# Reordering the attention work inside a fused decoder layer: scores, casts, row copies and meta rows at other steps

## The chip, the cores and the metric

The kernel runs on one core of a Trainium2 chip. The metric is the device time of one execution in microseconds (us). A core has a matmul engine (TensorE, PE in the profile; its weight loads are listed apart as PEld), a vector engine (DVE), a scalar engine (ACT), a general engine (POOL) and a queue for transfers (SP). Each of them works through its own list of instructions in order, and waits at an instruction until what it needs is there. SBUF is the working memory (rooms and raw, hi and lo buffers in the profile's names); PSUM holds the results of matmuls, and its eight banks are used here as four for sums that build up over many matmuls ("acc") and four for everything short ("ps").

## The reference

One step of one layer of a decoder, in float32, for a prompt of 512 tokens behind 16 meta tokens and for 8 running sequences of 4 new tokens each, which have 256 tokens in a paged cache:

```
h = x + 0.5 * rms_norm(swiglu(rms_norm(x), ffn1))
u = rms_norm(h);  proj = u @ w_in            # q,k,v,r and gates of both branches
o_a = gla(q_a, k_a, v_a, g)                  # gated linear attention, in chunks of 64
o_b = sb_attend(q_b, k_b, v_b, bias)         # stick-breaking attention, 16 heads of 64
m = sigmoid(gate_a) * (o_a @ w_o_gla) + sigmoid(gate_b) * (o_b @ w_o_sb)
h = h + rms_norm(m @ w_out)
y = h + 0.5 * rms_norm(swiglu(rms_norm(h), ffn2))

# sb_attend: z = q.k / 8 + bias, keys strictly before the query
# A[t,s] = sigmoid(z_ts) * prod over s<j<t of (1 - sigmoid(z_tj)),  out = A @ v
```

D_MODEL is 1024. Results are y for prompt and samples, the new rows of k and v, and the state of the linear attention.

## The kernel before, in words

**Products.** Every float32 operand of a large product is split into a high part (a cast, on ACT) and a low part (what is left, a subtraction on DVE, line 172). A product is then three matmuls: hi by hi, hi by lo, lo by hi. The wide projections are done with seven block products instead of eight (`seven_steps`, L1049 to L1084): the four accumulators a, d, b and c get sums of several products each, and two of them start from a copy of another: b from a, and c from b. These two copies (L1069, ACT) are called **seeds** here. Copies L1059 take intermediate values out of accumulators. The seven products come in the order a, d, b, d, c, a, c; their weights are four sets of blocks, named b1, t, b2 and t4, each with a cast (L1006 for hi) and a subtraction (lo) at dates that `weights_at` (L1041) hands out.

**Order.** PE, DVE, ACT and POOL run in an order that is written by hand; only SP's transfers are placed by the framework. The clock of that order is `step()` (L745), called once every six matmuls of a projection; `later(n, f)` does f n steps on. The attention has eight pairs of heads. Projections of pair p+1 take 22 steps: eight for the queries (L728 to L731), fourteen for keys and values (`seven_steps`, lines L1079 to L1081). The attention proper of pair p is laid between them, at step numbers that a table gives:

- `scores(n)` for three tiles of queries: six matmuls (L1997) into two PSUM banks, one for each head; a little later two sigmoids for each head out of the bank (L2004, L2005, ACT); POOL sets a few columns to zero.
- `scan` (L2021, DVE), the running product, and `weigh` (L172 and L2031, DVE), the weights, for two parts of the row and both heads: 815 columns for tiles 0 and 1, 528 for tile 2.
- `rows_k` and `rows_v`: k and v of the pair are turned (four transposes each, L2039 and L2054), copied out of PSUM (L2043 and L2058, both ACT) and sent out.
- `tails` (L2067 and on) and `turned` (L2096, copies L2099): the weights are transposed; `summed` (L2112) multiplies them with v; `meta_turned` (L2122, a cast L2123 on ACT and a subtraction on DVE) and `meta_summed` (L2127) add what the meta tokens give.
- In pairs 4 to 7 `sample_keys` (L2199, copies L2201) turns cached keys of the running sequences in four groups of four transposes, a PSUM bank each, and `sample_products` (L2213) multiplies with them. `sample_rows_out` (L2178) is done once.

The casts and subtractions of the next pair's queries (L1928 and on) are laid there too. After the pairs comes the mixer, whose value r is done by `seven_steps` again; `by_t` and `by_sg` work on its output (L2410), and `split` (L2352) casts it to hi.

**Rooms.** Most SBUF buffers come from one arena; where each `take` is put, a table of bytes says (PLACES, L53), one byte for each take in the order of the program. A room is taken anew as soon as `give` returned it, and the next writer waits for the last reader.

## Time and profile before

| | us |
|---|---|
| time, three runs | 1498.48, 1499.78, 1499.94 |
| median | 1499.78 |
| the profiled execution | 1498.65 |
| its span, first to last instruction | 1496.9 |
| PE busy in the span | 1477.6 |
| DVE, ACT, POOL busy | 1081.4, 804.8, 59.0 |

The attention pairs lie between about 587 and 825 us of the span; a plain pair's 22 steps take about 27.6 us, a pair with sample keys 32.1. In the profile a row of the timeline gives start, duration, engine, line, operation, output and input, the number of like instructions in a row, and in brackets the idle time of the engine just before it with what ended it. "PE ps L2199 <- ACT room L2043" in the list of waits is PE's line 2199, waiting for ACT's line 2043. Matmuls of 280 columns follow each other every 0.13 us, though each has a row of 0.29: their rows overlap.

### The profile page before, as it was taken

How to read it: one execution, taken by the hardware profiler on the slowest of the kernel's cores; microseconds unless marked ns; L12 is line 12 of the kernel's file. 1: busy time of each engine (PE TensorE's matmuls, PEld its weight loads, DVE VectorE, ACT ScalarE, POOL GpSimd, SP SyncE). 2: the span in 40 equal slices, each digit the busy share in tenths (PEclk: the TensorE clock that was granted, in tenths of full speed). 3: DMA queues.
4: the chain of work that ended last, by engine and by line, in shares of the span. 5: the costliest groups of instructions: out<-in, count | busy, mean ns of one | idle time of the engine just before them, and what ended most of it. 6: DMA issues, size and time to landing. Idle time of an engine off the chain costs nothing.

```text
span 1496.9 us, 29837 instructions
## 1 busy us (share of the span) xinstructions
PE 1477.6 (99%) x11905; PEld 1423.7 (95%) x11905; DVE 1081.4 (72%) x1820; ACT 804.8 (54%) x1513; POOL 59.0 (4%) x175
## 2 busy tenths in 40 slices
PE   9999999999999999999899999999999999999998
PEld 8999999999999889888789899999999999999998
DVE  5888888855676866877766844766567898888544
ACT  6455444533655656766766543644565555455333
POOL 2000000000000011200100000000000000000000
PEclk9999999999999999999999999999999999999999
DMA  8133333224655586556566857344531333333252
GB/s 252 51 91 100 99 96 102 86 79 139 164 138 142 158 157 163 118 125 131 129 126 169 245 139 212 90 103 129 171 103 66 99 100 99 99 101 94 82 174 93
DMA packets 288542, 187.61 MB, mean 125 GB/s; under 512 B 10989, under 2 KB 266675, under 8 KB 288403
## 3 DMA queue, kind: packets, MB, share of 16 engines
q1 hardware_dynamic: 280706, 181.97, 44.2%
q0 software_dynamic: 7680, 3.74, 2.4%
q8 instruction: 93, 1.52, 0.4%
q14 instruction: 47, 0.38, 0.1%
q10 hardware_dynamic: 16, 0.00, 0.0%
HBM read 160.63 MB, written 25.03 MB: 124 GB/s over the span
## 4 chain that ended last, share of the span: by engine, by line
PE 90%; DVE 3%; ACT 2%; DMA 2%; issue 1%; SPq 1%; DVEq 0%; ACTq 0%
PE acc L1300 8%; PE acc L1302 8%; PE acc L1301 8%; PE acc L741 6%; PE acc L742 6%; PE acc L744 6%; PE acc L728 5%; PE acc L729 4%; PE acc L731 4%; PE acc L1079 4%; PE acc L1081 3%; PE acc L1080 3%; DVE room L172 1%; PE acc L1242 1%; PE acc L1239 1%; PE acc L1240 1%
## 5 line engine op out<-in xcount | busy, mean ns | idle before, releaser
L172 DVE TENSOR_TENSOR room<-room,room 128x280 f32<-128x280 f32 (+13 forms) x462 | 288.2, 643 | 84.0 <-ACT room L808 18.3
L172 DVE TENSOR_TENSOR lo<-raw,hi 128x1024 fp32r<-128x1024 f32 (+1 forms) x207 | 248.1, 1199 | 98.0 <-ACT hi L1006 60.3
L1300 PE MATMUL acc<-room,hi 128*128 128x280 f32 (+1 forms) x896 | 260.0, 290 | 0.0
L1302 PE MATMUL acc<-room,lo 128*128 128x280 f32 (+1 forms) x896 | 259.7, 290 | 0.0
L1301 PE MATMUL acc<-room,hi 128*128 128x280 f32 (+1 forms) x896 | 259.5, 290 | 0.0
L1006 ACT CAST hi<-raw 128x1024 fp32r<-128x1024 f32 x114 | 119.6, 1053 | 141.5 <-PE acc L1301 49.5
L728 PE MATMUL acc<-room,hi 128*128 128x280 f32 x608 | 172.9, 301 | 0.3 <-DVE room L175 0.3
L1300 PEld LDWEIGHTS acc<-room,hi 128*128 128x128 f32 x896 | 168.7, 188 | 0.0
L1302 PEld LDWEIGHTS acc<-room,lo 128*128 128x128 f32 x896 | 168.6, 188 | 0.0
L1301 PEld LDWEIGHTS acc<-room,hi 128*128 128x128 f32 x896 | 168.6, 188 | 0.0
L729 PE MATMUL acc<-room,hi 128*128 128x280 f32 x608 | 163.6, 288 | 0.0
L1079 PE MATMUL acc<-room,hi 128*128 128x280 f32 x476 | 142.8, 300 | 3.2 <-ACT acc L1069 3.0
L172 DVE TENSOR_TENSOR lo<-room,hi 128x1024 fp32r<-128x1024 f32 x106 | 101.3, 955 | 56.5 <-ACT hi L1006 56.3
L1081 PE MATMUL acc<-room,lo 128*128 128x280 f32 (+1 forms) x476 | 138.6, 291 | 0.8 <-DVE lo L172 0.8
L1080 PE MATMUL acc<-room,hi 128*128 128x280 f32 (+1 forms) x476 | 138.4, 291 | 0.0
L706 ACT CAST hi<-raw 128x1024 fp32r<-128x1024 f32 (+1 forms) x93 | 93.6, 1007 | 74.4 <-issue 21.4
L1006 ACT CAST hi<-room 128x1024 fp32r<-128x1024 f32 x106 | 88.9, 839 | 82.3 <-PE acc L1301 60.1
L731 PE MATMUL acc<-room,lo 128*128 128x280 f32 x608 | 125.9, 288 | 0.0
L728 PEld LDWEIGHTS acc<-room,hi 128*128 128x128 f32 x608 | 114.4, 188 | 5.4 <-issue 3.8
L729 PEld LDWEIGHTS acc<-room,hi 128*128 128x128 f32 x608 | 114.6, 188 | 0.6
L741 PE MATMUL acc<-room,hi 128*128 128x280 f32 (+2 forms) x388 | 110.7, 295 | 0.0
L742 PE MATMUL acc<-room,hi 128*128 128x280 f32 (+2 forms) x388 | 108.8, 290 | 0.0
(404 smaller groups left out, 3515.8 us busy)
## 6 DMA issues: line engine op xcount, KB each, us to landing
raw<-in_w_in_dram SPq DMA_DIRECT2D x68, 256.0 KB, 5.2
raw<-in_ffn_w_gate_dram SPq DMA_DIRECT2D x64, 256.0 KB, 3.1
raw<-in_ffn_w_up_dram SPq DMA_DIRECT2D x64, 256.0 KB, 3.4
raw<-in_ffn_w_down_dram SPq DMA_DIRECT2D x36, 448.0 KB, 4.0
raw<-in_w_in_dram SPq DMA_DIRECT2D x29, 512.0 KB, 7.0
out_dram<-room SPq DMA_DIRECT2D x36, 256.0 KB, 6.2
room<-in_cache_k_dram SPq DMA_DIRECT2D x32, 256.0 KB, 6.7
room<-in_cache_v_dram SPq DMA_DIRECT2D x32, 256.0 KB, 5.2
```

Of the source, the lines that this page charges most:

```text
L172: (eng or V).tensor_tensor(out=out, in0=a, in1=b, op=op)
L728: T.matmul(acc[h][:, :w], hi[k], act.get(k, h, w)[0], start=(k == order[0]), stop=False, skip_group_check=True)
L729: T.matmul(acc[h][:, : wid[h]], hi[k], a[h][1], start=False, stop=False, skip_group_check=True)
L731: T.matmul(acc[h][:, : wid[h]], lo[k], a[h][0], start=False, stop=(k == order[-1]), skip_group_check=True)
L741: T.matmul(acc[h][:nw, : wid[h]], wh, a[h][0], start=(k == 0), stop=False)
L742: T.matmul(acc[h][:nw, : wid[h]], wh, a[h][1], start=False, stop=False)
L1006: S.copy(hi[:, :kt], src)
L1079: T.matmul(x[:, :n], hi, act_[k][0][:, :n], start=(first and k == 0), stop=False, skip_group_check=True)
L1081: T.matmul(x[:, :w], lo, act_[k][0][:, :w], start=False, stop=(k == 3), skip_group_check=True)
L1300: T.matmul(x[:, :QW], hi, act[k][0], start=(first and k == 0), stop=False, skip_group_check=True)
L1301: T.matmul(x[:, :QW], hi, act[k][1], start=False, stop=False, skip_group_check=True)
L1302: T.matmul(x[:, :QW], lo, act[k][0], start=False, stop=(k == 3), skip_group_check=True)
```

## The change

No instruction is added or taken away. The table of steps and a few dates change, the copy of the k rows goes from ACT to DVE, and the table of places is replaced as a whole.

```diff
-            for n, f in ((3, samples), (6, hi), (9, lo)):
+            for n, f in ((3, samples), (8, hi), (10, lo)):
...
         def rows_k(self):
...
                 kt = take(512)
-                S.copy(kt, p)
+                V.tensor_copy(kt, p)
...
-                later(4, lambda: give(kt))
-            later(3, out)
+                later(10, lambda: give(kt))
+            later(2, out)
...
         def rows_v(self):
...
-            later(4, out)
+            later(3, out)
...
         def meta_summed(self):
             T.matmul(self.op, once["vm"][:NR], once["az"][:NR], start=False, stop=True)
             o, pr = take(NP), self.pr
-            S.copy(o, self.op)
-            later(3, lambda: nc.sync.dma_start(ob_dram[pr], o))
-            later(7, lambda: give(o))
+            def out():
+                S.copy(o, self.op)
+                later(2, lambda: nc.sync.dma_start(ob_dram[pr], o))
+                later(6, lambda: give(o))
+            later(1, out)
...
         def by_sg(i):
             tt(o[i], o[i], sg[i], ALU.mult)
             give(t[i], sg[i])
-            split(oas, n + i, o[i], oap)
+            later(2, lambda: split(oas, n + i, o[i], oap))
...
-    SK, SP, TURN = (14, 14, 14, 14), (16, 16), (17, 17, 17, 20, 20, 20)
+    SK, SP, TURN = (14, 14, 14, 14), (19, 19), (16, 16, 16, 19, 19, 19)
...
-            now, n, after = Pair(pr), BEGIN[pr + 1], BEGIN[pr + 2] if pr < 7 else BEGIN[8] + 22
+            now, n, after = Pair(pr), BEGIN[pr + 1], BEGIN[pr + 2] if pr < 7 else BEGIN[8] + 21
             if pr >= PLAIN:
-                weights_at(then, BEGIN[pr] + TILE, ("kv", pr), (-6, -6, -5, -4), t=(-3, -2), b2=(2, 3), t4=(5, 7))
+                weights_at(then, BEGIN[pr] + TILE, ("kv", pr), (-6, -6, -5, -4), t=(-3, -1), b2=(0, 3), t4=(7, 9))
...
-            pieces = [(3, now.scores, 0), (3, now.scores, 1), (4, now.meta), (6, now.scan, 0, 0), (7, now.scan, 1, 0),
-                      (8, now.scan, 0, 1), (9, now.weigh, 0, 0), (10, now.scan, 1, 1), (12, now.weigh, 1, 0),
-                      (11, now.scores, 2), (11, now.rows_v), (11, now.rows_k),
-                      (14, now.scan, 0, 2), (15, now.weigh, 0, 1), (16, now.scan, 1, 2), (17, now.weigh, 1, 1), (17, now.tails)]
-            pieces += [(TURN[i], now.turned, i // 3, i % 3) for i in range(6)] + [(TURN[5], now.meta_turned)]
+            pieces = [(3, now.scores, 0), (3, now.scores, 1), (4, now.meta), (5, now.scan, 0, 0), (6, now.scan, 1, 0),
+                      (7, now.scan, 0, 1), (8, now.weigh, 0, 0), (9, now.scan, 1, 1), (11, now.weigh, 1, 0),
+                      (10, now.scores, 2), (10, now.rows_v), (10, now.rows_k),
+                      (12, now.scan, 0, 2), (13, now.weigh, 0, 1), (14, now.scan, 1, 2), (15, now.weigh, 1, 1), (16, now.tails)]
+            pieces += [(TURN[i], now.turned, i // 3, i % 3) for i in range(6)]
...
+            then(after + 1, now.meta_turned)
             then(after + 1, now.summed)
             then(after + 1, now.meta_summed)
...
-        then(BEGIN[2] + 14, sample_rows_out)
+        then(BEGIN[2] + 21, sample_rows_out)
```

Two places show what this makes of the engines' lists. The first is ACT in the pair at 699 to 731 us, the first one with sample keys, from the first seed (L1069) to the second. L2004 and L2005 are the sigmoids of the last tile, a couple for each head; L1059 copies the value e5; "ps" with a number is a PSUM bank. Before:

```order
L1069 COPY acc_8195<-acc_8193 128x280
L1006 CAST hi_8225<-raw_7900 128x1024
L1059 COPY room_76_4272<-acc_8194 128x280
L2004 ACTIVATE room_7_75<-ps_8238,sbb 128x512
L2005 ACTIVATE room_76_4272<-ps_8238,sbb 128x512
L2004 ACTIVATE room_79_4590<-ps_8239,sbb 128x512
L2005 ACTIVATE room_103_5552<-ps_8239,sbb 128x512
L1006 CAST hi_8282<-room_98_5485 128x512
L1928 CAST room_44_452<-room_60_3148 128x512
L1069 COPY acc_8196<-acc_8195 128x280
L1059 COPY room_75_4271<-acc_8195 128x280
L2043 COPY room_60_3148<-ps_8251 128x512
```

And now (L2205 is the line of the sample keys' copies, which was L2201):

```order
L1069 COPY acc_8202<-acc_8200 128x280
L2004 ACTIVATE room_91_5265<-ps_8230,sbb 128x512
L2005 ACTIVATE room_5_73<-ps_8230,sbb 128x512
L1059 COPY room_71_4267<-acc_8201 128x280
L2004 ACTIVATE room_71_4267<-ps_8231,sbb 128x512
L2005 ACTIVATE room_124_7976<-ps_8231,sbb 128x512
L2058 COPY room_9_112<-ps_8238 128x512
L1069 COPY acc_8203<-acc_8202 128x280
L1059 COPY room_124_7976<-acc_8202 128x280
L2205 COPY room_91_5265<-ps_8301 128x512
L2205 COPY room_99_5529<-ps_8307 128x512
L2205 COPY room_9_112<-ps_8313 128x512
```

The first head's sigmoids now stand ahead of L1059, the b2 cast (L1006, 128x1024) ahead of the first seed, and the casts L1006 (128x512, the t4 blocks) and L1928 behind the sample keys; L2058 stands where L2043 did not, ahead of the second seed, and L2043 has left this list.

The second place is DVE in the first pair, from the subtraction for the t blocks (lo, first row) to the scan of the last tile (128x528). Before:

```order
L172 TENSOR_TENSOR lo_6773<-room_86_4753,hi_6772 128x1024
L2021 SCALAR_TENSOR_TENSOR room_60_3148<-room_60_3148,room_74_4270 128x416
L2021 SCALAR_TENSOR_TENSOR room_104_5553<-room_104_5553,room_74_4270 128x400
L172 TENSOR_TENSOR room_103_5552<-room_103_5552,room_104_5553 128x815
L2031 COPY room_95_5301<-room_103_5552 128x6x16
L2021 SCALAR_TENSOR_TENSOR room_60_3148<-room_60_3148,room_74_4270 128x400
L1924 COPY room_94_5276<-room_98_5485 64x4x4 x4
L172 TENSOR_TENSOR lo_6824<-raw_6375,hi_6823 128x1024
L172 TENSOR_TENSOR room_79_4590<-room_79_4590,room_60_3148 128x815
L2031 COPY room_95_5301<-room_79_4590 128x6x16
L2021 SCALAR_TENSOR_TENSOR room_104_5553<-room_104_5553,room_74_4270 128x528
```

And now:

```order
L172 TENSOR_TENSOR lo_6774<-room_5_73,hi_6773 128x1024
L172 TENSOR_TENSOR room_9_112<-room_9_112,room_100_5549 128x815
L2031 COPY room_98_5501<-room_9_112 128x6x16
L2021 SCALAR_TENSOR_TENSOR room_71_4267<-room_71_4267,room_79_4672 128x400
L1924 COPY room_98_5501<-room_5_73 64x4x4 x4
L172 TENSOR_TENSOR room_49_871<-room_49_871,room_71_4267 128x815
L2031 COPY room_98_5501<-room_49_871 128x6x16
L172 TENSOR_TENSOR lo_6804<-raw_6375,hi_6803 128x1024
L2043 COPY room_99_5529<-ps_6839 128x512
L2021 SCALAR_TENSOR_TENSOR room_100_5549<-room_100_5549,room_79_4672 128x528
```

Two scans have gone ahead of the first row, the other head's 815-column product ahead of the second subtraction, and the k rows' copy L2043 stands behind that subtraction, ahead of the last tile's scan.

## The prediction

> **What bounds the kernel now.** I read the page's totals first, then PE's waits, then the timeline around each wait, on PE and on the engine that releases it.

> ```profile
> span 1496.9 us, 29837 instructions
> PE 1477.6 (99%) x11905; PEld 1423.7 (95%) x11905; DVE 1081.4 (72%) x1820; ACT 804.8 (54%) x1513; POOL 59.0 (4%) x175
> ```

> PE is busy 99% of the span. The change takes no instruction away from it, so it can give back only part of the 1496.9 − 1477.6 = 19.3 us in which PE stood idle, and what hides behind the busy figure. Which of that idle time belongs to the attention pairs, the list of PE's waits tells (columns: total us, times, longest):

> ```profile
> PE ps L2199 <- ACT room L2043: 4.4, 3, 1.5
> PE acc L1079 <- ACT acc L1069: 3.0, 3, 1.0
> PE ps L2199 <- ACT room L2005: 1.5, 3, 0.5
> PE acc L1081 <- DVE lo L172: 0.8, 1, 0.8
> PE ps L2122 <- DVE room L172: 0.6, 1, 0.6
> PE ps L2178 <- ACT room L2005: 0.2, 1, 0.2
> ```

> These are 10.5 us, and all of them have an instruction that the change moves as releaser. They are shown too small: a matmul's own row is longer than the pitch at which matmuls follow each other. So I measure each stall as distance between neighbours on PE, less what the distance would be undisturbed. First the sample-key transposes (L2199), which pairs 4 to 6 put into PE's stream:

> ```profile
> 711.52 0.29 PE L1081 MATMUL acc<-room,lo 128*128 128x280 f32 x1
> 711.92 0.66 PE L2199 MATMUL ps<-ident,room 128*128 128x128 f32 x4
> 713.07 0.66 PE L2199 MATMUL ps<-ident,room 128*128 128x128 f32 x4 [0.50 <-ACT room L2005]
> 715.19 1.14 PE L2199 MATMUL ps<-ident,room 128*128 128x128 f32 x8 [1.47 <-ACT room L2043]
> 716.09 0.37 PE L1079 MATMUL acc<-room,hi 128*128 128x280 f32 x1
> 716.31 0.29 PE L1080 MATMUL acc<-room,hi 128*128 128x280 f32 x1
> 716.44 0.29 PE L1081 MATMUL acc<-room,lo 128*128 128x280 f32 x1
> ```

> From the last projection matmul to the next are 716.09 − 711.52 = 4.57 us. Four transposes more make a group 1.14 − 0.66 = 0.48 longer, so sixteen need 1.92; with the pitch of 0.13 (716.44 − 716.31) and some 0.1 to enter the block that is 2.15. Lost: 2.4 us, three times. What holds them is ACT's queue:

> ```profile
> 710.30 0.39 ACT L1059 COPY room<-acc 128x280 f32<-128x280 f32 x1 [2.07 <-PE acc L1081]
> 710.59 0.69 ACT L2004 ACTIVATE room<-ps,sbb 128x512 f32<-128x512 f32 x1
> ...
> 712.31 0.71 ACT L2005 ACTIVATE room<-ps,sbb 128x512 f32<-128x512 f32 x1
> 712.88 0.65 ACT L1006 CAST hi<-room 128x512 fp32r<-128x512 f32 x1
> 713.39 0.66 ACT L1928 CAST room<-room 128x512 fp32r<-128x512 f32 x1
> 713.91 0.43 ACT L1069 COPY acc<-acc 128x280 f32<-128x280 f32 x1
> ...
> 714.51 0.63 ACT L2043 COPY room<-ps 128x512 f32<-128x512 f32 x1
> ```

> The reader should see the bracket in the first row: ACT stands 2.07 us idle in front of L1059, which needs a product that PE has not finished, with four sigmoids, two casts, the second seed (L1069) and the copy out of PSUM (L2043) lined up behind it. PE then waits for the end of that line, because the four PSUM banks of the scores and rows come free only there. Pairs 2 and 3 have no sample keys; there the same line ends in the seed, and PE waits for that:

> ```profile
> 657.75 0.29 PE L1081 MATMUL acc<-room,lo 128*128 128x280 f32 x1
> 659.08 0.40 PE L1079 MATMUL acc<-room,hi 128*128 128x280 f32 x1 [1.04 <-ACT acc L1069]
> ```

> 1.33 apart instead of 0.13: 1.20 lost, twice.

> **The change, part by part.** *Pairs 4 to 6.* The scores come one step of six matmuls earlier (0.78), and the first head's two sigmoids stand ahead of L1059, in the 2.07 idle us, which hold two at a pitch of 0.57. Behind L1059 remain two sigmoids, from 710.59 to about 711.8 with the second one's tail, then L2058 (the other rows copy) until about 712.4, then the seed. L2043 is no longer in this queue; DVE does it, at about 711. PE wants the four banks at 711.8, 712.2, 712.7 and 713.1 (0.48 a group). The tightest has some 0.3 us left. The casts L1006 and L1928 (0.5 each by their pitch) stand behind the seed, and their readers come four to five steps later. Term: 3 × −2.4 = **−7.2**, bounds −7.5 and, if one bank stays 0.5 late, −5.7.

> *Pairs 2 and 3.* Of what stood between L1059 and the seed, two sigmoids and two casts go (2.2 us) and one copy (0.5) comes: the seed starts near 657.0, ends near 657.4. It is also needed later, since tails and turned rows (L2067, L2096), once behind step 17, now precede its first matmul by well over 1 us. Term: 2 × −1.2 = **−2.4**, with 2 us in hand.

> *The first pair.* Its lost time hangs on DVE:

> ```profile
> 593.79 1.23 DVE L172 TENSOR_TENSOR lo<-room,hi 128x1024 fp32r<-128x1024 f32 x1 [2.24 <-ACT hi L1006]
> 594.94 1.90 DVE L2021 TENSOR_TENSOR_SCAN room<-room,room 128x416 f32<-128x416 f32 x2
> ...
> 599.46 1.22 DVE L172 TENSOR_TENSOR lo<-raw,hi 128x1024 fp32r<-128x1024 f32 x1
> ```

> PE waits 0.8 for the last row's subtraction and 0.6 for the meta rows (L2122); with the 0.16 that a row's length hides (1.20 lost against 1.04 shown, above) these are 0.96 and 0.76. The two scans move ahead of the earlier subtraction, into the 2.24 us that DVE is idle. The weights' product of the other head (1.0) comes ahead of the last subtraction in their place, so this one starts near 598.7 and ends near 599.9, 0.76 sooner: 0.2 remain. L2122 goes into the next pair's sums, where its rows are long finished: its 0.76 go. What is late next: the turned rows' fourth group needs the last tile's weights, and from 599.9 DVE's line of rows copy (0.6), scan (1.25) and product (0.7) ends near 602.45, where PE, by its new order, is ready near 601.95: +0.5. Term: −0.76 − 0.76 + 0.5 = **−1.0**, bounds −1.7 and +0.3.

> *Rows copy on DVE.* The trace has that shape on DVE:

> ```profile
> L2219 DVE COPY room<-ps x2: 666/669/672, 719.5 to 837.7; 128x512 f32<-128x512 f32 x2
> 671.80:699.40 27.60, 26.56 (x216) 24.14 (x214) 21.79 (x39) 19.09 (x38) 3.26 (x10) 1.00 0.82 154
> ```

> 0.67 us against ACT's 0.63. A pair's period (second row: length; PE, PEld, DVE, ACT, POOL busy) has DVE busy 21.79 of 27.60; 22.5 still fits. In pair 2 the line behind it is this, and it has the same durations in the first:

> ```profile
> 657.35 1.25 DVE L2021 TENSOR_TENSOR_SCAN room<-room,room 128x528 f32<-128x528 f32 x1
> 658.70 0.71 DVE L172 TENSOR_TENSOR room<-room,room 128x528 f32<-128x528 f32 x1
> ```

> Going through DVE's new order with these durations, this product ends at about 658.1 instead of 659.4; PE's fourth group wants it at about 658.4. I cost the copy at nothing; PE's early arrival is what could uncover it (rival two). [...]

> *The gate value r.* A seed of the mixer waits behind a cast that waits for DVE:

> ```profile
> 855.29 0.64 ACT L2352 CAST room<-room 128x544 fp32r<-128x544 f32 x1 [1.70 <-DVE room L172]
> 855.84 0.39 ACT L1069 COPY acc<-acc 128x280 f32<-128x280 f32 x1
> 856.28 0.40 PE L1079 MATMUL acc<-room,hi 128*128 128x280 f32 x1 [0.92 <-ACT acc L1069]
> ```

> The cast moves two steps back, behind that seed, which can then start when its source is there. Term: 0.92 and the hidden 0.16, **−1.1**.

> *Smaller ones.* The sample rows (L2178) go seven steps later: **−0.4** (0.2 shown, 0.16 of it hidden as above). The sample products join the second block of turned rows:

> ```profile
> 717.61 0.29 PE L1081 MATMUL acc<-room,lo 128*128 128x280 f32 x1
> 717.83 1.07 PE L2213 MATMUL ps<-room,room 128*32 128x256 f32 x16
> ```

> Entering a block costs 0.22 − 0.13 = 0.09, leaving it the same (716.31 − 716.09 = 0.22). Four blocks less: −0.7 at most, nothing at least; **−0.5**. The meta rows:

> ```profile
> L2123 ACT CAST room<-ps x8: 582/605/607, 609.7 to 821.0; 96x512 fp32r<-96x512 f32 x8
> 611.93 1.94 PE L2112 MATMUL ps<-room,room 128*64 128x512 f32 x10
> ```

> Between their transposes and the matmul that closes the sums PE now has L2112's sixteen, of which ten take 1.94; the cast (0.6) on ACT and a remainder on DVE, as wide as the 0.71 product at most, lie under them: nothing, as long as neither engine is in a longer piece just then. The lo, hi and t4 dates move by one or two steps under three or more of slack: nothing. DMAs: the same ones, earlier by a step; only a kept room (ten steps instead of four) could make a taker wait, and the new table of places goes with it: nothing, with a rival.

> *The clock.* Behind the third stall the windows show this (length; busy and counts of PE, PEld, DVE, ACT, POOL; clock; DMA):

> ```profile
> 775.90:779.30 3.40, 1.39 (x9) 0.84 (x8) 3.23 (x6) 3.40 (x9) 0.20 (x2) 1.00 0.20 42
> 779.30:782.80 3.50, 3.44 (x16) 3.44 (x17) 0.36 (x1) 2.64 (x6) 0.00 (x0) 0.52 0.20 66
> ```

> PE was busy 1.39 of 3.40 us, and in the next 3.5 the granted clock is 0.52: half the work, 1.7 us lost. The first two stalls were as long and had no such stretch. If the idle window goes, I expect the stretch to go with it: **−1.7**, bounds −1.7 and 0. [...]

> Sum: −7.2 − 2.4 − 1.0 − 1.1 − 0.4 − 0.5 − 1.7 = **−14.3 us**. The profiled execution took 1498.65 (span 1496.9 and 1.75 around it), so 1484.35. The median of the three runs is 1499.78, 1.13 higher; I predict against it: **1485.5 us**.

> **Rivals.** *One: the half-clock stretch stays,* or falls in another place. For: the granted clock fell once, and nothing above shows what decides; sixteen transposes in a row remain. Against: no other stretch in the pairs. 1485.5 + 1.7 = 1487.2.

> *Two: DVE's line becomes the releaser.* The waits on ACT go, but PE reaches the turned rows sooner than the last tile's weights, or the end of the sums sooner than the meta rows' remainder. For: 0.3 us in hand in pair 2, DVE 80% busy, one more copy in its line. Against: in pairs 4 to 6 the sample keys give it 2 us more. One lo subtraction of 1.23 in the wrong place, less 0.3 of slack, in seven pairs: 6.5 us back, 1492.

> *Three: part of the bank wait stays.* L2199 then waits for L2058 or the second head's sigmoids: 1.2 in each of three pairs, and the clock's 1.7 stay with it: 1490.8.

> *Four: nothing comes of it.* Rooms of the new table have their last reader later than the old ones, and what came sooner in the order waits for its room. For: the kept room, all places new. Against: every term above was a wait for a bank or for a queue, never for a room. 1499.

> *Five, slower: the rows copy blocks DVE.* It stands ahead of scan and weights and waits itself for PE and for a room that a transfer out reads. If it is held until the b lo and t4 lo subtractions behind it are late at L1081, PE waits in all eight pairs. It decides from about 3 us of delay, what the t4 piece has in hand (four steps of 0.78); for a loss over the 14.3 it must cost 1.8 a pair. At 2.2 a pair: 1485.5 + 17.6 = 1503. Against: its bank's matmuls (L2039) end over 1 us before DVE is there.

> **How the numbers follow.** Forecast 0.60 (its own range 1483 to 1488.5), rival one 0.13, two 0.11, three 0.07, four 0.05, five 0.04. The range must reach rivals one to three: 1482 to 1492; the lower end is the sum with all bounds on the good side (−0.3, −0.7, −0.2), a median no higher than the profiled execution (−1.1), and 1.2 for stalls that I counted too small. A measurement here can tell 0.2%, 3.0 us, from no change. The forecast and rivals one to three are all past that, 0.91, and a sliver of rival four: faster 0.92, same 0.04, slower 0.04.

> **What would show it.** In the changed profile the rows "L2199 <- L2043", "L2199 <- L2005" and "L1079 <- L1069" are missing from PE's waits, and L2199's sixteen stand together in about 2 us; ACT's idle in front of L1059 is under 1 us, with two sigmoids ahead of it; no slice between 700 and 860 us has a clock of 0.5. If PE shows waits of L2096 for DVE in more than the first pair, rival two is right; L2199 with waits of about 1 us, rival three; the same waits as now, four; L1081 waiting for L172 in most pairs, five. I am wrong if PE's idle time falls by under 6 us.

## The result, and the profile after

The changed kernel takes 1483.04 us (median of four runs, 1482.95 to 1483.10); the kernel before, in four runs beside it, 1499.13 (1498.35 to 1499.94). The ratio is 0.9893, with a 95% interval of 0.9875 to 0.9910: 16.1 us faster. The forecast was 1485.5 us, in a range of 1482 to 1492.

The first rows of the changed kernel's page, and from its list of PE's waits the two in the upper rows that are new:

```profile
span 1481.4 us, 29840 instructions
PE 1472.0 (99%) x11905; PEld 1421.1 (96%) x11905; DVE 1086.3 (73%) x1828; ACT 800.6 (54%) x1505; POOL 57.7 (4%) x175
...
PE acc L744 <- DVE lo L172: 0.7, 1, 0.7
PE ps L2096 <- DVE room L172: 0.7, 2, 0.4
```

PE's idle time in the span went from 19.3 to 9.4 us, its busy time from 1477.6 to 1472.0. All six waits that the prediction showed are gone from the list, and two small new ones are there. A pair with sample keys looks so now, on PE and then on ACT (line numbers behind L2126 have grown by 4):

```profile
708.01 0.29 PE L1081 MATMUL acc<-room,lo 128*128 128x280 f32 x1
708.14 1.91 PE L2203 MATMUL ps<-ident,room 128*128 128x128 f32 x16
709.80 0.38 PE L1079 MATMUL acc<-room,hi 128*128 128x280 f32 x1
```

```profile
704.29 0.69 ACT L2004 ACTIVATE room<-ps,sbb 128x512 f32<-128x512 f32 x1 [0.34 <-PE ps L1997]
704.87 0.68 ACT L2005 ACTIVATE room<-ps,sbb 128x512 f32<-128x512 f32 x1
706.80 0.39 ACT L1059 COPY room<-acc 128x280 f32<-128x280 f32 x1 [1.25 <-PE acc L1081]
707.09 0.69 ACT L2004 ACTIVATE room<-ps,sbb 128x512 f32<-128x512 f32 x1
707.67 0.69 ACT L2005 ACTIVATE room<-ps,sbb 128x512 f32<-128x512 f32 x1
708.24 0.59 ACT L2058 COPY room<-ps 128x512 f32<-128x512 f32 x1
708.71 0.42 ACT L1069 COPY acc<-acc 128x280 f32<-128x280 f32 x1
```

The first head's sigmoids stand where ACT had been idle for 2.07 us, and the sixteen transposes run through in one piece: 709.80 − 708.01 = 1.79 us from matmul to matmul, where it was 4.57. Two of the prediction's signs came out otherwise: ACT still stands idle for 1.25 us in front of L1059, where under 1 was expected, and L2096 waits for DVE in two pairs, which was the sign of rival two.

**A ledger.** Times of whole runs hide where a microsecond comes from. Both traces have the same 9357 accumulating matmuls in the same order, so I compared when the same matmul starts. What the changed kernel gains between two of them, in us:

| stretch | gain |
|---|---|
| start to the first pair (0 to 568 us) | −0.63 |
| pair 0, pair 1 | +1.51, −0.05 |
| pair 2, pair 3 | +1.32, +1.31 |
| pairs 4, 5, 6 | +2.86, +2.76, +4.36 |
| pair 7 | +0.15 |
| r, to 869 us | +1.20 |
| the rest | +0.44 |
| sum | +15.2 |

Pair n's row is the period in which its attention is done. The same ledger was made for each experiment below. It is sharper than the times: with one and the same program text up to there, the changed kernel starts a cast (L706) at 373.49 us, and three variants of it start the same one at 374.28, 374.39 and 375.37 (k rows on ACT, early t4 cast, early sample products). A run's time has such distances in it, and the ledger shows them apart from the edit.

### The profile page after: what moved, and what is told of

The parts are those of the page before. It is cut to its first block, busy times and chain, and to the rows that moved or that the text cites. A ratio compares the mean times of both kernels' runs of the same rounds, so it can differ in the third digit from the quotient of the medians.

```text
span 1481.4 us, 29840 instructions
## 1 busy us (share of the span) xinstructions
PE 1472.0 (99%) x11905; PEld 1421.1 (96%) x11905; DVE 1086.3 (73%) x1828; ACT 800.6 (54%) x1505; POOL 57.7 (4%) x175
## 4 chain that ended last, share of the span: by engine, by line
PE 93%; DVE 3%; DMA 1%; ACT 1%; issue 1%; DVEq 0%; SPq 0%; ACTq 0%
PE acc L1300 8%; PE acc L1301 8%; PE acc L1302 8%; PE acc L741 7%; PE acc L744 6%; PE acc L742 6%; PE acc L728 5%; PE acc L729 4%; PE acc L731 4%; PE acc L1079 4%; PE acc L1080 4%; PE acc L1081 4%; PE acc L1242 2%; PE acc L1239 2%; PE acc L1240 2%; DVE room L172 1%
## 5 line engine op out<-in xcount | busy, mean ns | idle before, releaser
L172 DVE TENSOR_TENSOR room<-room,room 128x544 f32<-128x544 f32 (+12 forms) x469 | 293.0, 643 | 78.1 <-ACT room L1059 19.2
L172 DVE TENSOR_TENSOR lo<-raw,hi 128x1024 fp32r<-128x1024 f32 (+1 forms) x207 | 247.8, 1198 | 91.4 <-ACT hi L1006 54.4
L1006 ACT CAST hi<-raw 128x1024 fp32r<-128x1024 f32 x114 | 119.9, 1055 | 142.8 <-PE acc L1301 47.2
L1079 PE MATMUL acc<-room,hi 128*128 128x280 f32 x476 | 141.7, 298 | 0.3 <-ACT room L1059 0.3
L1080 PE MATMUL acc<-room,hi 128*128 128x280 f32 (+1 forms) x476 | 138.3, 290 | 0.0
L1081 PE MATMUL acc<-room,lo 128*128 128x280 f32 (+1 forms) x476 | 138.1, 290 | 0.1
L706 ACT CAST hi<-raw 128x1024 fp32r<-128x1024 f32 (+1 forms) x93 | 93.6, 1007 | 77.0 <-issue 20.4
L172 DVE TENSOR_TENSOR lo<-room,hi 128x1024 fp32r<-128x1024 f32 x106 | 101.1, 954 | 44.9 <-ACT hi L1006 44.7
L1006 ACT CAST hi<-room 128x1024 fp32r<-128x1024 f32 x106 | 89.2, 841 | 81.9 <-PE acc L1301 59.7
```

What stands on the lines that cost most here:

```text
L172: (eng or V).tensor_tensor(out=out, in0=a, in1=b, op=op)
L1006: S.copy(hi[:, :kt], src)
L1079: T.matmul(x[:, :n], hi, act_[k][0][:, :n], start=(first and k == 0), stop=False, skip_group_check=True)
L1080: T.matmul(x[:, :w], hi, act_[k][1][:, :w], start=False, stop=False, skip_group_check=True)
L1081: T.matmul(x[:, :w], lo, act_[k][0][:, :w], start=False, stop=(k == 3), skip_group_check=True)
```

## The experiments

My theory: before the change PE waited for the end of ACT's line, so each piece taken out of that line, or put behind the seed, gives back its length until something else is last. The rivals: the copy of the k rows on DVE is the cure; DVE becomes the releaser; the rooms or transfers matter. The first four runs do one part of the change on the kernel before.

**Scores one step earlier.**

```diff
-                      (11, now.scores, 2), (11, now.rows_v), (11, now.rows_k),
+                      (10, now.scores, 2), (11, now.rows_v), (11, now.rows_k),
```

> The kernel before, with one date changed: the last tile's scores come at step 10 instead of 11, so that the first head's two sigmoids stand ahead of L1059 on ACT; casts, rows copies and everything else stay. Theory (ACT's queue order sets the end): two sigmoids at a pitch of 0.57 leave the line behind L1059, so whatever stands behind them comes 1.15 us sooner: the seed's stall in pairs 2 and 3 shrinks from 1.3 to about 0.15, the three sample-key stretches on PE from 4.57 to about 3.4 us; in all -5.8 us, and -1.7 more if the half-clock stretch goes. Rival (the rows copy on DVE is what frees the bank): the sample-key stretches stay at 4.5, in all at most -2.4.

1494.45 us, against 1500.33 for the kernel before beside it. The sample-key stretches fell from 4.57 (the third one, with the half clock, from 5.25) to 3.42, 3.43 and 3.42: right. In pair 4, from 711.98 to 715.40:

```profile
711.98 0.29 PE L1081 MATMUL acc<-room,lo 128*128 128x280 f32 x1
712.11 1.04 PE L2199 MATMUL ps<-ident,room 128*128 128x128 f32 x8
714.50 1.15 PE L2199 MATMUL ps<-ident,room 128*128 128x128 f32 x8 [1.35 <-ACT room L2043]
715.40 0.38 PE L1079 MATMUL acc<-room,hi 128*128 128x280 f32 x1
```

Ledger: 1.12, 1.07 and 2.67 in pairs 4 to 6, the last with a half-clock stretch (1.55) less. But pairs 2 and 3 gained nothing (within 0.02): wrong. Pair 2 on DVE and then PE, in this run:

```profile
664.13 0.28 DVE L2076 COPY room<-ps 48x128 f32<-48x128 f32 x1
...
664.84 0.29 DVE L172 TENSOR_TENSOR room<-ps,room 32x128 fp32r<-32x128 f32 x1
```

```profile
663.06 1.52 PE L2096 MATMUL ps<-ident,room 128*128 128x128 f32 x10
665.18 0.64 PE L2122 MATMUL ps<-ident,room 128*96 128x128 f32 x4 [0.60 <-DVE room L172]
```

The seed's wait is gone, and L2122 stands until 665.18, just behind 664.84 + 0.29: DVE's last reading of the bank that holds the tails (L2076 to L172, "room<-ps"). PE gets there 1.1 us sooner, and waits 1.1 us more for DVE. (The numbers behind "ps" in the lists of the change count the tiles, not the four banks that hold them.)

**The copy of the k rows on DVE, alone.**

```diff
-                S.copy(kt, p)
+                V.tensor_copy(kt, p)
```

> The kernel before, with only the copy of the k rows moved from ACT to DVE, at its old step. Theory (queue order): the bank of L2043 is free about 2 us sooner, but the next group of four transposes then waits for the first copy of L2199's own results on ACT, behind seed and L1059 as before: sample-key stretch from 4.57 to about 4.0, pairs 2 and 3 unchanged (1.3 lost each), in all -1.5 us. Rival (this copy is the cure): the stretch falls to about 2, in all -7.5.

1499.43 us. The stretches are 4.09 each (0.49, 0.48 and, with a half-clock stretch gone, 2.03 gained), pairs 0, 2 and 3 lose 0.6 to 0.7, and pair 1 loses 1.75. No loss was expected in any of them. Pair 1:

```profile
629.24 0.29 PE L1081 MATMUL acc<-room,lo 128*128 128x280 f32 x1
631.76 0.21 PE L2178 MATMUL ps<-ident,room 32*128 32x32 f32 x1 [2.23 <-DVE room L2043]
```

On DVE the copy's bank comes free later for the sample rows: L2178 waits 2.23 us for it, where the kernel before shows 0.20, for ACT. So this part is not the cure; alone it costs more (3.7 us in pairs 0 to 3) than it gives (1.5 in pairs 4 to 6, without the half-clock stretch).

**The cast of the queries behind the seed, alone.**

```diff
-                S.copy(self.qs[0], qf[:, :NP])
+                later(2, lambda: S.copy(self.qs[0], qf[:, :NP]))
```

> The kernel before, with only the cast L1928 (0.52 by its pitch) two steps later, behind the second seed. Theory: every stall behind it on ACT shrinks by 0.52: in pairs 2 and 3 from 1.3 to 0.8, sample-key stretches from 4.57 to 4.05, in all -2.6 us. Rival (the casts don't matter, PE waits for the sigmoids' banks): nothing.

1497.01 us. Stretches of 4.06 and 4.05 (the middle one 4.78, with half the clock): 0.5 each, as expected. Pairs 2 and 3: 0.03 and 0.00, where 0.5 each was expected; L2122's wait took it here as well.

**The meta rows with the sums, alone.**

```diff
-            pieces += [(TURN[i], now.turned, i // 3, i % 3) for i in range(6)] + [(TURN[5], now.meta_turned)]
+            pieces += [(TURN[i], now.turned, i // 3, i % 3) for i in range(6)]
...
+            then(after + 1, now.meta_turned)
             then(after + 1, now.summed)
```

> The kernel before, with only the meta rows' transposes L2122 moved from the second block of turned rows to the next pair's sums. Theory: PE's block of turned rows in the first pair falls from 2.52 to 1.14 us and the sums' block rises from 2.86 to 3.30; in the other pairs 1.58 to 1.14 and 2.86 to 3.30, so nothing; in all -0.94 us. Rival (the meta rows' copies are late at the end of the sums now): the sums' block rises above 3.3 in several pairs and the gain is eaten up.

1499.21 us. Ledger: 0.76 in pair 0, where 0.94 was expected, 0.24 in pair 1, 0.02 and 0.03 in pairs 2 and 3. The sums' blocks are 3.29 or 3.30 in all pairs, so nothing is late at their end. The run's whole time says nothing here, since it has two half-clock stretches instead of one.

**Both.** If the wait of pairs 2 and 3 only changes its place, two parts together must give what neither gives alone.

> The kernel before, with two parts of the change: the last tile's scores at step 10, and the meta rows' transposes with the next pair's sums. Alone, the first gave 0.00 in pairs 2 and 3 (L2122 then waited for DVE) and the second 0.02. Theory (the wait had only moved from ACT's seed to DVE's weights): together they give 1.1 to 1.2 us in each of the two pairs, and the sample-key blocks stay at 3.4. Rival (DVE is late for the turned rows L2096 too, so that only earlier scans help): under 0.3 in each of the two pairs, with waits of L2096 for DVE.

1491.74 us (before: 1500.23). Pair 2 gained 0.79 and pair 3 0.22, where 1.1 to 1.2 each was expected. So the two give together what neither gives alone, but they aren't enough. The seed gives its 1.14 in both pairs, but the second block of turned rows takes 1.40 and 1.44 instead of 1.14, since it now waits for DVE, and in pair 3 the sums wait for the meta rows' remainder on DVE:

```profile
693.03 2.38 PE L2112 MATMUL ps<-room,room 128*64 128x512 f32 x16
695.87 0.50 PE L2127 MATMUL ps<-room,room 96*128 96x512 f32 x1 [0.46 <-DVE room L172]
```

The changed kernel has 1.3 in both, with DVE's scans earlier as well. That the scans make up the difference is argued from what is left over, and not shown: they were not moved alone, nor were the dates of the t and b2 weights or the copy of the v rows.

**The cast of r, alone.**

```diff
-    def split(dst, k, src, kept):
+    def split(dst, k, src, kept, lag=0):
...
-        S.copy(hi[:, :NW], src)
+        later(lag, lambda: S.copy(hi[:, :NW], src)) if lag else S.copy(hi[:, :NW], src)
...
-            split(oas, n + i, o[i], oap)
+            split(oas, n + i, o[i], oap, 2)
```

> The kernel before, with only the cast L2352 of r two steps later, behind the seed. Theory: 1.1 to 1.2 us less between 825 and 870 us, and nothing elsewhere. Rival (the subtraction that follows the cast becomes late for its own product): under 0.5.

Ledger: +1.19 in that stretch, 0.00 or 0.01 elsewhere but for 1.55 lost to a second half-clock stretch in pair 5 and 1.2 before the pairs; so the run's time (1500.03) shows nothing of it.

The other runs undo parts of the changed kernel, or add to it.

**The meta rows back behind the turned rows.**

```diff
-            pieces += [(TURN[i], now.turned, i // 3, i % 3) for i in range(6)]
+            pieces += [(TURN[i], now.turned, i // 3, i % 3) for i in range(6)] + [(TURN[5], now.meta_turned)]
...
-            then(after + 1, now.meta_turned)
```

> The changed kernel, with the meta rows' transposes back behind the second block of turned rows. Theory: in the changed profile DVE's last copy for the meta rows (L2031) ends 605.6 us into the first pair and PE would ask for it at 607.2, so with the earlier scans nothing waits, and this part of the change is worth nothing beside the others: the pairs take as long as now, within 0.1 us each. Rival (the move is what freed the pairs from DVE): 0.8 in the first pair and 1.0 in pairs 2 and 3 come back.

1485.89 us. The rival was right in kind: 0.73, 0.74, 0.33 and 0.42 us are lost again in pairs 0 to 3, and nothing in pairs 4 to 7. My expectation had asked for the wrong instruction. Pair 0 on DVE and PE:

```profile
606.23 0.21 DVE L2031 COPY room<-room 128x96 f32<-128x96 f32 x1
...
608.62 0.29 DVE L172 TENSOR_TENSOR room<-ps,room 32x128 fp32r<-32x128 f32 x1
```

```profile
608.96 0.64 PE L2122 MATMUL ps<-ident,room 128*96 128x128 f32 x4 [0.55 <-DVE room L172]
```

The rows to be transposed (L2031) are there at 606.44; L2122 starts at 608.96, behind DVE's last reading of the tails' bank (608.91). It waits for room in PSUM, not for its data.

**The t4 cast ahead of the seed again.**

```diff
-                weights_at(then, BEGIN[pr] + TILE, ("kv", pr), (-6, -6, -5, -4), t=(-3, -1), b2=(0, 3), t4=(7, 9))
+                weights_at(then, BEGIN[pr] + TILE, ("kv", pr), (-6, -6, -5, -4), t=(-3, -1), b2=(0, 3), t4=(5, 7))
```

> The changed kernel, with the t4 cast (L1006, 128x512) two steps earlier, ahead of the second seed, where it was. Theory: L2058 stands ahead of it, so banks for the sample keys are free as before; the seed comes 0.5 later and has over 0.5 in hand: nothing, within 0.3 us of 1483.0. Rival (each cast ahead of the seed costs its length wherever there are sample keys): four times 0.5, 1485.

1483.86 us; but by the ledger 0.90 of it is lost before the first pair, and at most 0.01 in any pair. The theory holds: this date is worth nothing once the other parts are in.

**The sample products before the tails again.**

```diff
-    SK, SP, TURN = (14, 14, 14, 14), (19, 19), (16, 16, 16, 19, 19, 19)
+    SK, SP, TURN = (14, 14, 14, 14), (16, 16), (16, 16, 16, 19, 19, 19)
```

> The changed kernel, with the sample products back at step 16, in front of the tails, instead of behind the second block of turned rows. The prediction's term says +0.5 us (four blocks more to enter and leave). Rival, from the blocks of the two traces (1.21 for the products alone and 1.14 for the turned rows alone, 2.31 for both together, while a block takes the place of one matmul's pitch of 0.13): nothing, within 0.3 us of 1483.0.

1484.86 us. Pairs 4 to 7 lose 0.07, 0.73, 0.13 and 0.07, in all 1.0; another 1.9 went in the profiled execution before the first pair, where the edit has no part. Neither expectation met it: at step 16 the products join the first block of turned rows, and in pair 5 they wait there for a bank that ACT's copies of turned rows hold:

```profile
743.03 1.25 PE L2096 MATMUL ps<-ident,room 128*128 128x128 f32 x10
744.98 1.07 PE L2217 MATMUL ps<-room,room 128*32 128x256 f32 x16 [0.69 <-ACT room L2099]
```

**The k rows back on ACT,** in all pairs, and in the pairs without sample keys alone.

```diff
-                V.tensor_copy(kt, p)
+                S.copy(kt, p)
```

> The changed kernel, with the copy of the k rows back on ACT, at its new step, where it stands between the second head's sigmoids and L2058. Theory: DVE's line is 0.6 shorter, so the two waits of turned rows (L2096, 0.53 and 0.51 lost in the first two pairs) go: -0.9 us; L2058 comes 0.47 later on ACT, where it has about 0.15 in hand, so each sample-key block (1.79 now) grows by 0.1 to 0.35 in pairs 4 to 7: +0.4 to +1.4. Between 1482.5 and 1483.5 us. Rival (DVE's line isn't what L2096 waits for): the waits stay and the time is 1483.5 to 1484.5.

```diff
-                V.tensor_copy(kt, p)
+                (S.copy if self.pr < 4 else V.tensor_copy)(kt, p)
```

> The changed kernel, with the copy of the k rows on ACT in pairs 0 to 3, which have no sample keys, and on DVE in pairs 4 to 7. Theory: the waits of L2096 in the first two pairs go and the sample-key blocks stay at 1.79: 1483.0 - 0.9 = 1482.1 us, faster than the changed kernel. Rival: the seed of pairs 0 to 3 becomes late behind the copy on ACT (L1079 waits for L1069): 1483 or more.

1482.71 (1482.59 to 1482.98) and 1482.63 us (1482.57 to 1483.01). In both, the waits of L2096 are gone: 0.62 and 0.56 gained in pairs 0 and 1 by the one, 0.59 and 0.57 by the other, and 0.00 in all other pairs. The loss that I expected from the first in pairs 4 to 7 didn't come; its blocks are 1.79 and 1.80 there. ACT in pair 4 of that run:

```profile
707.80 0.59 ACT L2043 COPY room<-ps 128x512 f32<-128x512 f32 x1
708.26 0.62 ACT L2058 COPY room<-ps 128x512 f32<-128x512 f32 x1
```

PE's first group starts there at 707.69, and the fourth starts 1.31 us later, at 709.00, just when L2058 has ended (708.88). So in the changed kernel nothing needs the copy on DVE. What it does cost, DVE's and PE's rows of the changed kernel show in pair 0, where PE has done three of the turned rows and then waits for the product that stands behind copy and scan:

```profile
600.48 0.69 DVE L2043 COPY room<-ps 128x512 f32<-128x512 f32 x1
601.08 1.25 DVE L2021 TENSOR_TENSOR_SCAN room<-room,room 128x528 f32<-128x528 f32 x1
602.43 0.71 DVE L172 TENSOR_TENSOR room<-room,room 128x528 f32<-128x528 f32 x1
```

```profile
602.34 0.49 PE L2096 MATMUL ps<-ident,room 128*128 128x128 f32 x3
603.20 0.98 PE L2096 MATMUL ps<-ident,room 128*128 128x128 f32 x7 [0.36 <-DVE room L172]
```

**A load that became free too early.** The changed kernel lost 0.9 to 1.0 us at 375 us, far ahead of the attention. Its SP queue, and PE there:

```profile
363.21 0.37 SPq L679 DMA_DIRECT2D room<-in_w_in_dram  x1
363.67 0.93 SPq L1346 DMA_DIRECT2D room<-h_dram  x2
365.88 0.38 SPq L205 DMA_DIRECT2D raw<-in_ffn_w_down_dram  x1
```

```profile
375.86 0.39 PE L744 MATMUL acc<-room,lo 128*128 128x280 f32 x1 [0.73 <-DVE lo L172]
```

In the kernel before, L679 is issued at 374.1. The down weight behind it then comes later; its cast waits for the transfer, first in the kernel before and then in the changed one:

```profile
371.31 1.05 ACT L706 CAST hi<-raw 128x1024 fp32r<-128x1024 f32 x1 [1.60 <-DMA raw<-in_ffn_w_down_dram]
```

```profile
373.49 1.05 ACT L706 CAST hi<-raw 128x1024 fp32r<-128x1024 f32 x1 [4.47 <-DMA raw<-in_ffn_w_down_dram]
```

Of the change, only the new table of places reaches so far ahead of the attention. That the load's old room was in use until 374, and that its new one is free sooner, is argued from this and shown by no trace. The experiment ties it to a small write by DVE, and has the k rows on ACT:

```diff
             self.early[r0, c0] = room = take(8 * P)
-            nc.sync.dma_start(room.rearrange("p (k n) -> p k n", n=2 * P),
+            def load():
+                V.memset(room[:, :1], 0.0)
+                nc.sync.dma_start(room.rearrange("p (k n) -> p k n", n=2 * P),
...
+            later(8, load)
...
-                V.tensor_copy(kt, p)
+                S.copy(kt, p)
```

> The changed kernel with the copy of the k rows on ACT in all pairs, and with one load (L679, an early piece of the projection weights, 512 KB) tied to a one-column write of DVE in its room eight steps later, so that it can't be issued before. In the changed kernel this load is issued at 363 us, in the one before at 374, and a down weight landed some 2 us later behind it, for which PE waited 0.73 (L744). Theory (the new table of places set that load free too early): the wait of L744 goes, 0.9 us less before the pairs than with the k rows on ACT alone: about 1481.8 us. Rival (the h loads between the weights, not this one, make it late): the wait stays, 1482.7.

1481.46 us (1480.94 to 1481.58; ratio to the kernel before 0.9874, interval 0.9858 to 0.9891). The wait of L744 is gone, with 1.0 us gained at that matmul, and 0.59 and 0.57 in pairs 0 and 1. It is the fastest kernel of this case: by the ledger 1.60 us ahead of the changed kernel, by the medians 1.58.

## Why the prediction was right, and where not

**Pairs 4 to 6** (−7.2). The mechanism was right and the size too small: the blocks fell by 2.78 each (the third without its half clock), 8.3 in all. The step that failed is the undisturbed length. I built it from differences of groups and got 2.15, so 2.4 lost. The same sixteen transposes stood undisturbed in the trace of before, in pair 7, where no seed follows:

```profile
809.32 1.93 PE L2199 MATMUL ps<-ident,room 128*128 128x128 f32 x16
811.01 0.38 PE L728 MATMUL acc<-room,hi 128*128 128x280 f32 x1
```

Its neighbours are 1.81 apart; in the changed kernel they are 1.79 or 1.80 apart in all four pairs. Of the 2.78, the scores' step gave 1.1, the queries' cast 0.5 and the k rows 0.5 when done alone; with the 0.5 of the t4 cast by its pitch that is 2.6. The t4 cast was not tried alone on the kernel before. That the parts nearly add up supports one line on one engine as the cause. They overlap at the end: with the rest in place, neither the t4 date nor the copy on DVE is needed.

**Pairs 2 and 3** (−2.4): 2.63, the right sum with a gap in the reason. I had let PE wait for the seed alone. The runs showed a second wait right behind, L2122 for the tails' bank, that takes back whatever the seed gives; "2 us in hand" held for the seed only. The meta rows' move, to which I gave a gain in pair 0 alone ("nothing" in the others), is worth 0.3 to 0.4 here.

**Pair 0** (−1.0): 1.51. The new +0.5 was there (0.53 over the pitch), and L1081's wait gave back 0.75, as forecast. L2122's was worth more than I had it at: its block fell from 2.52 to 1.14 while the sums grew by 0.44, which is 0.94 instead of 0.76. The first matmul behind a wait loses another 0.1 to the second one, which I had left out: in pair 2 of the kernel before the next one after 659.08 starts at 659.31, 0.23 later against a pitch of 0.13. Two small waits of the kernel before stood in no term: its first block of turned rows took 1.62, where it takes 1.47 in pairs 1 to 3, and the matmuls at 602.25 and 602.48 came 0.22 late together. The reason I gave for L2122, that its rows are finished by then, is wrong: it waited for a bank.

**Pair 1** (−0.4 for the sample rows): −0.05. The block of the sample rows fell from 1.59 to 1.26, as expected. What failed is "I cost the copy at nothing": the wait that I had put into the first pair comes here too (0.51 over the pitch, 0.35 of it shown). This is rival two, in two pairs out of the seven and with 0.6 instead of 0.9 each. The copy itself takes a little longer on DVE than on ACT: 0.69 − 0.63 = 0.06 by the median durations of the two profiles, 0.60 − 0.46 = 0.14 by the distance to the next row's start (600.48 to 601.08 on DVE, 707.80 to 708.26 on ACT). But what costs is the place in DVE's line, 0.6 in each of the two pairs.

**r** (−1.1): 1.19 alone, 1.20 in the change. **The sample products** (−0.5): nothing. Products and second turned rows together are 2.31; apart they were 1.22 and, without L2122's 0.44, 1.14, each less one pitch of 0.13 that the matmul behind has anyway: 2.10 against 2.18. So the step that failed is that a block saved is time saved: together they take no less than apart.

**The clock** (−1.7): 1.55, and gone in the changed kernel and in every variant of it. That the stretch would go with the stall was an expectation from one stretch in one trace. The runs bear it out: none follows the six blocks of 3.4 us, nor the changed kernel's four of 1.79 or 1.80. Rival one fell.

**Transfers** ("the same ones, earlier by a step", nothing): wrong by 0.9 to 1.0 us. I put the table of places down as a risk of waits for rooms, and it cost through a load that came sooner. It is not rival four, which had rooms come free later. Rivals three, four and five did not occur.

So the sum of 14.3 was 1 us short of the ledger's 15.2: +1.1 (blocks), +0.2 (pairs 2 and 3), +0.5 (pair 0), −0.45 (pair 1), +0.1 (r), −0.5 (products) and −0.15 (clock) make 15.1, and pair 7, what lies before the pairs, the load included, and what lies behind r cancel out (+0.15 − 0.63 + 0.44). Terms missed by up to 1 us have cancelled as well: the range held, but not because each step did. The time lies 2.5 us below the forecast for one more reason: I had added 1.13 because the median before lay above its profiled execution, and in the changed kernel the two are the same (1483.04 and 1483.06).

## What to carry to other kernels

Before you estimate what a stall costs, look for the same block without the stall in the same trace: the difference of the two lengths is the price (here 4.57 − 1.81 us). When one engine's queue is the releaser, ask for each stretch which wait comes right behind the one you remove, and for a "ps" wait ask who still reads the bank, not whether the data are ready. Read a table of places as a table of transfer dates: where a room is free earlier, a load may be issued earlier, and it can be in the way far from the change (here L679, at 363.21 us instead of 374.1, with a wait of 0.73 on PE at 375.86).

## What the runs showed of the hardware

A half-clock stretch follows some long stalls on PE, and not others of the same length. From the run with the meta rows moved alone, behind its first sample-key stall:

```profile
715.87 0.58 PE L1079 MATMUL acc<-room,hi 128*128 128x280 f32 x1
...
717.42 0.43 PE L1079 MATMUL acc<-room,hi 128*128 128x280 f32 x1
717.65 0.43 PE L1080 MATMUL acc<-room,hi 128*128 128x280 f32 x1
...
718.35 0.31 PE L1080 MATMUL acc<-room,hi 128*128 128x280 f32 x1
718.50 0.29 PE L1081 MATMUL acc<-room,lo 128*128 128x280 f32 x1
```

The matmuls are 0.23 apart instead of 0.13 until 718.35. In the seven traces of the kernel before and of single parts of it there are 21 sample-key blocks in pairs 4 to 6. Of the fifteen that lasted over 4 us six were followed or overtaken by such a stretch, of the six of 3.4 us none; each cost about 1.55 us by the ledger.

```profile
711.57:714.98 3.41, 1.44 (x12) 0.97 (x10) 3.13 (x6) 3.41 (x9) 2.03 (x3) 1.00 0.36 96
714.98:718.39 3.41, 3.41 (x18) 3.34 (x17) 0.00 (x0) 2.09 (x5) 0.64 (x1) 0.50 0.73 130
779.83:783.24 3.41, 1.95 (x17) 1.64 (x15) 2.06 (x4) 3.41 (x9) 0.00 (x0) 1.00 0.35 77
783.24:786.65 3.41, 3.41 (x36) 2.65 (x35) 2.11 (x4) 0.87 (x2) 0.00 (x0) 1.00 0.48 148
```

PE was busy 42% of the window ahead of the half clock, and 57% of the other. Of the 21 blocks, take the window in which PE is least busy: the half clock follows all five windows with 41 to 47%, one of the three with 48 to 55%, and none of the thirteen with 57% and more. What decides between 47 and 57%, these runs leave open.

The kernel before had one such stretch in its profiled execution, other kernels of that kind none, one or two. That fits its runs' spread, 1498.35 to 1502.52 us, and the changed kernel's, 1482.95 to 1483.10, which has no such stall. The executions that were only timed left no trace, but their mean granted clock is on record: of the fourteen of the kernel before beside the experiments, the two at 0.999 took 1498.55 and 1499.05, the ten at 0.998 and 0.997 took 1499.63 to 1500.71, and the two at 0.996 took 1501.42 and 1502.52. One stretch lowers the mean by 0.5 × 3.41 / 1497 = 0.0011. This bears the link out, without showing the single stretches.
